# Fixed residues modulo 256 bytes for the large SBUF buffers of a one-core decoder step

## The chip, the cores and the metric

The kernel runs on one core of one Trainium2 chip. The metric is device time in microseconds (us) of one execution. TensorE (PE) does the matrix products; its weight loads are listed apart (PEld). VectorE (DVE), ScalarE (ACT) and GpSimd (POOL) do the element-wise work, and SyncE (SP) issues most of the DMAs.

## The reference

One layer of a hybrid decoder trunk on 256 prompt tokens and 64 sample tokens, 320 columns in all, in float32:

```python
h = rms_norm(x, attn_norm_g); z = h @ w_in       # [u | v | glu_a | glu_b | q | gates]
y_a = (gelu(u) * (tril(sgu_w) @ LN(gelu(v)) + sgu_b)) @ w_a_out
y_b = silu(LN(causal_dwconv(glu_a * sigmoid(glu_b)))) @ w_b_out
y_c = cross_attention(q, mem_k, mem_v) @ w_c_out
x = x + (g_A * y_a + g_B * y_b + g_C * y_c) @ w_o          # g = sigmoid(gates + b_gate)
x = x + square(relu(rms_norm(x, mlp_norm_g) @ w_up)) @ w_down
y = rms_norm(x, final_norm_g)
```

D_MODEL is 2048, the branches are 1024 wide and the MLP 8192. The keys and values of the prompt's memory come from `rms_norm(mem) @ w_mem_kv` (the "kv" stage); those of the samples are read from a cache. New keys and values, convolution states and the samples' normalised v rows are outputs too.

## The kernel before

Activations are held transposed, channels on the partitions and the 320 tokens along the row. Every large product takes float32 operands apart into a rounded part ("hi", type fp32r) and a remainder ("lo"), and adds three matmuls for each product of two 128-blocks: hi weights by hi activations, hi weights by lo activations, lo weights by hi activations. This document calls them a triple. They stand at L1307, L1308 and L1309 of the main loop, each with its own load of a 128x128 block of weights and 320 columns of activations as the moving operand:

```python
nc.tensor.matmul(a, hi[:, k, ms], xh, start=(kk == 0), stop=False)
nc.tensor.matmul(a, hi[:, k, ms], xl, start=False, stop=False)
nc.tensor.matmul(a, lo[:, k, ms], xh, start=False, stop=(last and k == 1))
```

The weights pass once, in 544 "halves" of 256 rows by 512 columns (512 KB). For each half, `load_to` (L199) has SP load a raw tile `wraw` (three buffers), ACT rounds it into `whi` (L222 where the norm's gain is multiplied in, L248 elsewhere) and DVE writes the remainder `wlo` (through the wrapper at L43); three buffers each. One half of a "T" product (512 of the 544) is four output blocks by two k-blocks, so eight triples, 24 matmuls. The other 32 halves are the kv stage (L1337 to L1339), where the weights are the moving operand, 512 columns, and the transposed memory `mh`/`ml` is loaded as the stationary one. The order of the stages is fixed by the list of groups: glu, q, kv, gate C, u, v, w_c_out, gate A with w_a_out, gate B with w_b_out, w_o, and then four times w_up and w_down. All other work (transposes, convolution taps on DVE, attention, norms) is put between the matmuls by hand, by half (`side`, `after`, `pace`), and the tile framework adds the semaphores.

Which buffers `operand` (L1021) gives as xh and xl depends on the stage: `hh`/`hl` for w_in and w_up, `ob` for w_c_out, `ya` for w_a_out, `yb` for w_b_out, `moh`/`mol` for w_o, `ah`/`al` for w_down. Under w_o, k-blocks 0 to 7 of `mol` lie in tag T5, and 8 to 15 in T7 (L1105).

Tiles come from one pool. A tag gets its place at its first use, one behind the other, each size rounded up to 32 bytes per partition, from byte 16,512 of the partition on. A row of 320 floats is 1280 bytes, five times 256, and blocks of weights start 512 bytes apart, so every operand of a matmul has the residue of its tile's start modulo 256. From the order and sizes in the program they are, before:

| buffers | tag | first byte | mod 256 |
|---|---|---|---|
| wraw | wraw | 61312 | 128 |
| hh, hl | HH, HL | 75232, 95712 | 224, 224 |
| whi, wlo | whi, wlo | 116192, 128480 | 224, 224 |
| ah, mh | T1 | 20352 | 128 |
| ya, ob (hi and lo), ml | T2 | 40832 | 128 |
| al, yb (hi, lo) | T4a, T4b | 177792, 188032 | 128, 128 |
| moh | T3a, T3b | 147072, 157312 | 128, 128 |
| mol, k-blocks 0 to 7 | T5 | 216096 | 32 |
| mol, k-blocks 8 to 15 | T7 | 205728 | 160 |

Of the kernel before, what the change touches and what calls it, by code (L numbers as in the profile page):

```python
# [10 lines left out]
F32R = mybir.dt.float32r  # L11
# [9 lines left out]
EPS = 1e-6  # L21
CONV_PACE = 0.75
WARM = 5
QUARTER = (0, 1)


# [22 lines left out]
def decoder_step_kernel(  # L49
# [26 lines left out]

    def tmp():
        return sb([128, NT], "tr", bufs=3)

    def f32(ap):  # L80
        return ap.bitcast(F32)
# [310 lines left out]
    def conv_setup():  # L392
        ident = S["ident"]
        cx = [sb([128, 4, 590], "T3a", name="cx0"), sb([128, 4, 590], "T3b", name="cx1")]
        S["cx"] = cx
        S["dc"] = sb([128, 8, NT], "T6", name="dc")
        hist = sb([120, 2, 1024], "T4a", name="hist")
        cwn = sb([31, 1024], "T4b", name="cwn")
        for g in range(2):
            nc.sync.dma_start(  # L400
                hist[:, g], state_conv[0, 4 * g:4 * g + 4].rearrange("b t c -> (b t) c")
            )
        nc.sync.dma_start(cwn, conv_w[0])
        nc.sync.dma_start(out_hist_s[0, :, 0:14, :], state_conv[0, :, 8:22, :])
        for t in cx:
            nc.gpsimd.memset(t[:, :, 0:30], 0.0)
        cw = sb([128, 8, 31], "cw")
        S["cw"] = cw
        steps = []

        def cw_step():
            p = ps_misc([128, 8, 64])
            for ct in range(8):
                nc.tensor.transpose(
                    p[:, ct, :31], cwn[:, 128 * ct:128 * (ct + 1)], ident[:31, :31]
                )
            nc.scalar.activation(cw, p[:, :, :31], AF.Copy)

        steps.append(cw_step)

        def hist_step(ct):
            p = ps_misc([128, 2, 256])
            for g in range(2):
                nc.tensor.transpose(
                    p[:, g, :120], hist[:, g, 128 * ct:128 * (ct + 1)], ident[:120, :120]
                )
            dst = cx[ct // 4][:, ct % 4, 286:590].rearrange("p (b w) -> p b w", w=38)
            for g in range(2):
                nc.scalar.activation(
                    dst[:, 4 * g:4 * g + 4, 0:30],  # L430
                    p[:, g, :120].rearrange("p (b t) -> p b t", t=30), AF.Copy,
                )

        for ct in range(8):
            steps.append(lambda ct=ct: hist_step(ct))
        return steps
# [113 lines left out]

    def yb_step(c):
        if c == 0:
            S["yb"] = [sb([128, 8, NT], t, F32R, name="yb") for t in ("T4a", "T4b")]
        split(S["yb"][0][:, c], S["yb"][1][:, c], S["dc"][:, c])


# [121 lines left out]
    def ya_step(g):  # L678
        if g == 0:
            flush()  # L680
            S["ya"] = sb([128, 2, 8, NT], "T2", F32R, name="ya")
        split(S["ya"][:, 0, g], S["ya"][:, 1, g], S["u"][:, g])


    def mem_load(i):
# [25 lines left out]

    def mem_tr_step(k):
        if k == 0:
            S["mh"] = sb([128, 16, 256], "T1", F32R, name="mh")
            S["ml"] = sb([128, 16, 256], "T2", F32R, name="ml")
        p = ps_misc([128, 2, 256])
        for t in range(2):
            nc.tensor.transpose(
                p[:, 0, 128 * t:128 * (t + 1)],
                S["mem"][k // 8][:, t, 128 * (k % 8):128 * (k % 8 + 1)], S["ident"],  # L720
            )
        split_scaled(S["mh"][:, k], S["ml"][:, k], p[:, 0], col("mem_g", k))
# [10 lines left out]
    def attn_prompt_steps(h):  # L733
        st = {}
        kt = (2 * h, 2 * h + 1)

        def scores():
            if h == 0:
                S["ob"] = sb([128, 2, 8, NT], "T2", F32R, name="ob")
            st["sc"] = ps_misc([128, 2, 256])  # L740
            for t in range(2):
                for j in range(2):
                    nc.tensor.matmul(  # L743
                        st["sc"][:, t], S["q"][:, kt[j], 128 * t:128 * (t + 1)],
                        S["kT"][:, kt[j]], start=(j == 0), stop=(j == 1),
                    )
            after(1, peak)
            after(2, soft)
            after(3, scale)

        def peak():
            mx = sb([128, 2], "mx", bufs=2)
            V.reduce_max(mx, st["sc"], axis=AX.X)
            st["nb"] = sb([128, 2], "nb", bufs=2)
            V.tensor_scalar(st["nb"], mx, -1.0 / 16, None, op0=ALU.mult)

        def soft():
            st["p"] = sb([128, 2, 256], "at", bufs=3)
            st["sm"] = sb([128, 2], "sm", bufs=2)
            for t in range(2):  # L760
                nc.scalar.activation(
                    st["p"][:, t], st["sc"][:, t], AF.Exp, bias=st["nb"][:, t:t + 1],
                    scale=1.0 / 16, accum_out=st["sm"][:, t:t + 1],
                )

        def scale():
            r = sb([128, 2], "rr", bufs=2)
            V.reciprocal(r, st["sm"])
            for t in range(2):
                V.tensor_scalar(st["p"][:, t], st["p"][:, t], r[:, t:t + 1], None, op0=ALU.mult)  # L770

        def tr():
            pp = ps_misc([128, 2, 256])
            for mt in range(2):
                for t in range(2):
                    nc.tensor.transpose(
                        pp[:, mt, 128 * t:128 * (t + 1)],
                        st["p"][:, t, 128 * mt:128 * (mt + 1)], S["ident"],
                    )
            st["pT"] = sb([128, 2, 256], "at", bufs=3)  # L780
            nc.scalar.activation(st["pT"], pp, AF.Copy)

        def pv():
            o = ps_misc([128, 2, 256])
            for j in range(2):
                for mt in range(2):
                    nc.tensor.matmul(  # L787
                        o[:, j], S["vn"][:, mt, 128 * kt[j]:128 * (kt[j] + 1)],
                        st["pT"][:, mt], start=(mt == 0), stop=(mt == 1),
                    )  # L790
            split(S["ob"][:, 0, 2 * h:2 * h + 2, 0:NP], S["ob"][:, 1, 2 * h:2 * h + 2, 0:NP], o)

        return [scores, tr, pv]

# [26 lines left out]
    def attn_sample_steps(g):  # L821
# [17 lines left out]
        def scores(b):  # L839
            sc = ps_misc([128, 512])  # L840
            for j in range(2):
                for h in range(4):
                    nc.tensor.matmul(  # L843
                        sc[32 * h:32 * h + 32, 0:256],
                        S["q"][:, 2 * h + j, NP + 32 * g:NP + 32 * g + 32],
                        st["kT"][:, 2 * h + j], start=(j == 0), stop=(j == 1),
                    )
            nb = sb([128, 2], "nb", bufs=2)
            sm = sb([128, 2], "sm", bufs=2)
            p = st["p"] = tmp()  # L850

            def peak():
                mx = sb([128, 2], "mx", bufs=2)
                V.reduce_max(mx[:, 0:1], sc[:, 0:256], axis=AX.X)
                V.tensor_scalar(nb[:, 0:1], mx[:, 0:1], -1.0 / 16, None, op0=ALU.mult)

            def soft():
                nc.scalar.activation(
                    p[:, 0:256], sc[:, 0:256], AF.Exp, bias=nb[:, 0:1], scale=1.0 / 16,
                    accum_out=sm[:, 0:1],  # L860
                )

            def scale():
                r = sb([128, 2], "rr", bufs=2)
                V.reciprocal(r[:, 0:1], sm[:, 0:1])
                V.tensor_scalar(
                    p[:, 0:256], p[:, 0:256], r[:, 0:1], S["mask"][:, b % 4:b % 4 + 1],
                    op0=ALU.mult, op1=ALU.mult,
                )

            after(1, peak)
            after(2, soft)
            after(3, scale)
# [31 lines left out]
        def fin():  # L905
# [5 lines left out]
            ob = S["ob"]  # L911
            for j in range(2):
                src = pp[:, j, 0:128].rearrange("p (h c) -> p h c", h=4)
                hi = ob[:, 0].rearrange("p (h j) t -> p h j t", j=2)[:, :, j, NP + 32 * g:NP + 32 * g + 32]
                lo = ob[:, 1].rearrange("p (h j) t -> p h j t", j=2)[:, :, j, NP + 32 * g:NP + 32 * g + 32]
                split(hi, lo, src)

        def T(b):
# [102 lines left out]
    def operand(key, kk):  # L1021
        kind = key[0]
        if kind in ("wA", "wC"):
            t = S[{"wA": "ya", "wC": "ob"}[kind]]
            return t[:, 0, kk], t[:, 1, kk]
        if kind == "wB":
            return S["yb"][0][:, kk], S["yb"][1][:, kk]
        if kind == "wo":
# [152 lines left out]


    with tc.manual_schedule():
        prologue()
        f = first

# [200 lines left out]
```

## Time and profile before

| what | value |
|---|---|
| median of 3 runs | 1999.29 us (1999.1 to 2005.92) |
| the profiled execution | 2000.53 us, of which its span is 1998.8 us |
| PE busy / PEld busy | 1976.0 us / 1933.9 us |
| DVE / ACT / POOL busy | 1194.4 / 821.0 / 32.7 us |
| HBM read | 311.48 MB, 159 GB/s over the span |

The page of the profile shows one profiled execution: busy time by engine, the span in 40 slices, the chain of work that ended last, and groups of instructions. The end of a matmul is modelled, so its duration (309 ns) says little; what a matmul costs in a dense stretch is the distance from its start to the next one's. That distance can be read in the list of instructions in order of time.

### The profile page before, as it was taken

Reading aid. Unit: us, or ns where it says so; the run is one execution under the profiler, and the core shown is the slowest. Engines: PE = TensorE matmul, PEld = TensorE weight load, DVE = VectorE, ACT = ScalarE, POOL = GpSimd, SP = SyncE. Lnnn points to the kernel's source line nnn. Section 1 sums busy time; section 2 is a strip of 40 time slices with the busy share of each in tenths; the row PEclk is TensorE's granted clock in tenths of the full one; section 3 lists DMA queues with packets and bytes.
Section 4 is the critical chain, followed back from the end, with each engine's and each line's share of the span. In section 5 each row is a group of like instructions: output and inputs, shape, how many; then the busy total and the mean of one; then the engine's idle time right before and its main releaser. Section 6 shows DMA issues by size and latency. Waiting matters only on the chain.

```text
span 1998.8 us, 32448 instructions
## 1 busy us (share of the span) xinstructions
PE 1976.0 (99%) x13316; PEld 1933.9 (97%) x13316; DVE 1194.4 (60%) x2079; ACT 821.0 (41%) x1185; POOL 32.7 (2%) x64
## 2 busy tenths in 40 slices
PE   9999999999999999999999999999999999999997
PEld 8999889889999999999999999999999999999997
DVE  5687787677788868655656554345434554445444
ACT  6454444445433445444444332233322333233332
POOL 0001000000200000000000000000000000000000
PEclk9999999999999999999999999999999999999998
DMA  6654665987644454544445544444444444444443
GB/s 212 192 148 141 208 200 121 208 225 205 217 150 136 148 150 146 152 156 151 139 162 168 152 144 149 158 149 147 149 157 148 149 142 153 158 148 147 145 152 106
DMA packets 189587, 319.25 MB, mean 160 GB/s; under 512 B 43377, under 2 KB 44105, under 8 KB 189302
## 3 DMA queue, kind: packets, MB, share of 16 engines
q1 hardware_dynamic: 184798, 302.56, 49.8%
q0 software_dynamic: 4640, 14.62, 2.1%
q8 instruction: 104, 1.70, 0.4%
q14 instruction: 45, 0.37, 0.1%
HBM read 311.48 MB, written 6.09 MB: 159 GB/s over the span
## 4 chain that ended last, share of the span: by engine, by line
PE 95%; DMA 2%; DVE 1%; ACT 0%; issue 0%; SPq 0%; DVEq 0%; ACTq 0%; POOLq 0%
PE acc L1307 29%; PE acc L1309 29%; PE acc L1308 29%; PE acc L1339 2%; PE acc L1338 1%; PE acc L1337 1%; DMA cache<-in_cache_mem_v_dram 1%; DMA wraw<-in_w_in_dram 1%; DVE wlo L43 0%; DMA cache<-in_cache_mem_k_dram 0%; PE misc L339 0%; PE misc L787 0%; PE misc L743 0%; PE misc L843 0%; PE acc L1285 0%; PE misc L893 0%
## 5 line engine op out<-in xcount | busy, mean ns | idle before, releaser
L1307 PE MATMUL acc<-hh,whi 128*128 128x320 f32 x2424 | 758.9, 313 | 0.0
L1309 PE MATMUL acc<-hh,wlo 128*128 128x320 f32 x2424 | 749.7, 309 | 0.0
L1308 PE MATMUL acc<-hl,whi 128*128 128x320 f32 x2424 | 749.6, 309 | 0.0
L43 DVE TENSOR_TENSOR wlo<-wraw,whi 128x1024 fp32r<-128x1024 f32 x368 | 448.7, 1222 | 427.4 <-ACT whi L248 427.3
L248 ACT ACTIVATE whi<-wraw 128x1024 fp32r<-128x1024 f32 x368 | 389.1, 1057 | 703.6 <-PE acc L1308 586.6
L1307 PEld LDWEIGHTS acc<-hh,whi 128*128 128x128 f32 x2424 | 455.8, 188 | 8.0 <-issue 6.6
L1308 PEld LDWEIGHTS acc<-hl,whi 128*128 128x128 f32 x2424 | 456.0, 188 | 0.4
L1309 PEld LDWEIGHTS acc<-hh,wlo 128*128 128x128 f32 x2424 | 455.6, 188 | 0.0
L222 ACT ACTIVATE whi<-wraw,vecs 128x512 fp32r<-128x512 f32 x352 | 236.5, 719 | 281.1 <-PE acc L1308 185.6
L1307 PE MATMUL acc<-ah,whi 128*128 128x320 f32 x1024 | 317.1, 310 | 0.0
L1308 PE MATMUL acc<-al,whi 128*128 128x320 f32 x1024 | 316.2, 309 | 0.0
L1309 PE MATMUL acc<-ah,wlo 128*128 128x320 f32 x1024 | 316.2, 309 | 0.0
L43 DVE SCALAR_TENSOR_TENSOR wlo<-wraw,vecs,whi 128x512 fp32r<-128x512 f32 x352 | 247.3, 745 | 71.2 <-ACT whi L222 70.4
L1308 PEld LDWEIGHTS acc<-al,whi 128*128 128x128 f32 x1024 | 192.5, 188 | 0.0
L1307 PEld LDWEIGHTS acc<-ah,whi 128*128 128x128 f32 x1024 | 192.5, 188 | 0.0
L1309 PEld LDWEIGHTS acc<-ah,wlo 128*128 128x128 f32 x1024 | 192.5, 188 | 0.0
L43 DVE SCALAR_TENSOR_TENSOR dc<-cx,cw,dc 128x256 f32<-128x256 f32 x480 | 153.0, 377 | 0.0
L43 DVE TENSOR_TENSOR res<-res,acc 128x320 f32<-128x320 f32 x80 | 39.0, 487 | 68.4 <-PE acc L1309 68.3
L1309 PE MATMUL acc<-moh,wlo 128*128 128x320 f32 x256 | 78.9, 308 | 0.0
L1307 PE MATMUL acc<-moh,whi 128*128 128x320 f32 x256 | 78.8, 308 | 0.0
L1308 PE MATMUL acc<-mol,whi 128*128 128x320 f32 x256 | 78.2, 306 | 0.0
L1039 ACT ACTIVATE ah<-tr 128x320 fp32r<-128x320 f32 x64 | 30.2, 472 | 67.3 <-DVE tr L43 67.3
(243 smaller groups left out, 1699.7 us busy)
## 6 DMA issues: line engine op xcount, KB each, us to landing
wraw<-in_w_in_dram SPq DMA_DIRECT2D x175, 512.0 KB, 4.0
wraw<-in_w_up_dram SPq DMA_DIRECT2D x128, 512.0 KB, 3.8
wraw<-in_w_down_dram SPq DMA_DIRECT2D x128, 512.0 KB, 3.6
wraw<-in_w_mem_kv_dram SPq DMA_DIRECT2D x32, 512.0 KB, 3.7
wraw<-in_w_o_dram SPq DMA_DIRECT2D x32, 512.0 KB, 3.7
cache<-in_cache_mem_k_dram SPq DMA_DIRECT2D x32, 256.0 KB, 6.4
cache<-in_cache_mem_v_dram POOLq DMA_DIRECT2D x8, 1024.0 KB, 7.3
wraw<-in_w_c_out_dram SPq DMA_DIRECT2D x16, 512.0 KB, 3.6
```

Source lines behind the costliest of these rows:

```text
L43: return fn(*args, **kw)
L222: nc.scalar.activation(hi, t, AF.Copy, scale=col("attn_g", 2 * h + k))
L248: nc.scalar.activation(parts[j][0], parts[j][1], AF.Copy)
L1039: nc.scalar.activation(out, in_, fn, **kw)
L1307: nc.tensor.matmul(a, hi[:, k, ms], xh, start=(kk == 0), stop=False)
L1308: nc.tensor.matmul(a, hi[:, k, ms], xl, start=False, stop=False)
L1309: nc.tensor.matmul(a, lo[:, k, ms], xh, start=False, stop=(last and k == 1))
L1337: nc.tensor.matmul(accs[t], mh, hi[:, k], start=(kk == 0), stop=False)
L1338: nc.tensor.matmul(accs[t], mh, lo[:, k], start=False, stop=False)
L1339: nc.tensor.matmul(accs[t], ml, hi[:, k], start=False, stop=(last and k == 1))
```

## The change

A new function `place` takes the large tags first, in a fixed order, right at the beginning, so that each keeps a chosen residue. Two helpers put a pad between the halves of a tile that holds hi and lo (40 floats, 160 bytes) or ahead of a hi part in a tag for lo ones (24 floats, 96 bytes). The small tiles of the softmax (`mx`, `nb`, `sm`, `rr`) become four parts of one tile `soft`, and the convolution's weights `cw` share the tag `rstd`. No instruction is added or removed by these edits.

```diff
+LO_HI, HI_LO, MEM_OFF = 40, 24, 0
...
+    def block(tag, name, off=0):
+        flat = sb([128, 8 * NT + off], tag, F32R, name=name)
+        return flat[:, off:].rearrange("p (k t) -> p k t", t=NT)
+    def both(tag, name):
+        flat = sb([128, 16 * NT + LO_HI], tag, F32R, name=name)
+        return [
+            flat[:, o:o + 8 * NT].rearrange("p (k t) -> p k t", t=NT)
+            for o in (0, 8 * NT + LO_HI)
+        ]
+    def mem_block(tag, name):
+        flat = sb([128, 16 * 256 + MEM_OFF], tag, F32R, name=name)
+        return flat[:, MEM_OFF:].rearrange("p (k t) -> p k t", t=256)
+    def place():
+        for tag, n, bufs in (
+            ("xss", 24, 1), ("whi", 1024, 3), ("wlo", 1024, 3), ("soft", 8, 2),
+            ("HL", 16 * NT, 1), ("T5", 8 * NT, 1), ("T7", 8 * NT, 1), ("T4b", 8 * NT, 1),
+            ("T4a", 8 * NT + HI_LO, 1), ("HH", 16 * NT, 1), ("T1", 16 * NT, 1),
+            ("T3a", 8 * NT, 1), ("T3b", 8 * NT, 1), ("T6", 8 * NT, 1),
+            ("T2", 16 * NT + LO_HI, 1),
+        ):
+            sb([128, n], tag, bufs=bufs, name="place")
...
-        cw = sb([128, 8, 31], "cw")
+        cw = sb([128, 8, 31], "rstd")
...
-            S["yb"] = [sb([128, 8, NT], t, F32R, name="yb") for t in ("T4a", "T4b")]
+            S["yb"] = [block("T4a", "yb", HI_LO), block("T4b", "yb")]
...
-            S["ya"] = sb([128, 2, 8, NT], "T2", F32R, name="ya")
-        split(S["ya"][:, 0, g], S["ya"][:, 1, g], S["u"][:, g])
+            S["ya"] = both("T2", "ya")
+        split(S["ya"][0][:, g], S["ya"][1][:, g], S["u"][:, g])
...
-            S["mh"] = sb([128, 16, 256], "T1", F32R, name="mh")
-            S["ml"] = sb([128, 16, 256], "T2", F32R, name="ml")
+            S["mh"] = mem_block("T1", "mh")
+            S["ml"] = mem_block("T2", "ml")
...
-                S["ob"] = sb([128, 2, 8, NT], "T2", F32R, name="ob")
+                S["ob"] = both("T2", "ob")
...
-            mx = sb([128, 2], "mx", bufs=2)
+            st["q"] = sb([128, 4, 2], "soft", bufs=2)
+            mx, st["nb"] = st["q"][:, 0], st["q"][:, 1]
...
     with tc.manual_schedule():
+        place()
         prologue()
```

Worked out from these sizes in the same way, the residues after are 224 for `whi` and `wlo` (bytes 16608 and 28896), 32 for `hl` (41248), T5, T7, T4b and T4a (61728, 71968, 82208, 92448; `yb`'s hi part begins 96 bytes into T4a, at 128), 128 for `hh` (102784), T1 (123264), T3a and T3b (143744, 153984) and T2 (174464), whose lo part begins at 184864, residue 32. `wraw` comes behind them and moves from residue 128 to 32.

More of the change, by code (lines that the diff above doesn't have):

```diff
@@ L751, in peak @@
         def peak():
-            mx = sb([128, 2], "mx", bufs=2)
+            st["q"] = sb([128, 4, 2], "soft", bufs=2)
+            mx, st["nb"] = st["q"][:, 0], st["q"][:, 1]
             V.reduce_max(mx, st["sc"], axis=AX.X)
-            st["nb"] = sb([128, 2], "nb", bufs=2)
             V.tensor_scalar(st["nb"], mx, -1.0 / 16, None, op0=ALU.mult)
@@ L758, in soft @@
             st["p"] = sb([128, 2, 256], "at", bufs=3)
-            st["sm"] = sb([128, 2], "sm", bufs=2)
+            st["sm"] = st["q"][:, 2]
             for t in range(2):
@@ L766, in scale @@
         def scale():
-            r = sb([128, 2], "rr", bufs=2)
+            r = st["q"][:, 3]
             V.reciprocal(r, st["sm"])
@@ L790, in pv @@
                     )
-            split(S["ob"][:, 0, 2 * h:2 * h + 2, 0:NP], S["ob"][:, 1, 2 * h:2 * h + 2, 0:NP], o)
+            split(S["ob"][0][:, 2 * h:2 * h + 2, 0:NP], S["ob"][1][:, 2 * h:2 * h + 2, 0:NP], o)
         return [scores, tr, pv]
@@ L847, in scores @@
                     )
-            nb = sb([128, 2], "nb", bufs=2)
-            sm = sb([128, 2], "sm", bufs=2)
+            q = sb([128, 4, 2], "soft", bufs=2)
+            mx, nb, sm, r = (q[:, i] for i in range(4))
             p = st["p"] = tmp()
             def peak():
-                mx = sb([128, 2], "mx", bufs=2)
                 V.reduce_max(mx[:, 0:1], sc[:, 0:256], axis=AX.X)
@@ L863, in scale @@
             def scale():
-                r = sb([128, 2], "rr", bufs=2)
                 V.reciprocal(r[:, 0:1], sm[:, 0:1])
@@ L913, in fin @@
                 src = pp[:, j, 0:128].rearrange("p (h c) -> p h c", h=4)
-                hi = ob[:, 0].rearrange("p (h j) t -> p h j t", j=2)[:, :, j, NP + 32 * g:NP + 32 * g + 32]
-                lo = ob[:, 1].rearrange("p (h j) t -> p h j t", j=2)[:, :, j, NP + 32 * g:NP + 32 * g + 32]
+                hi = ob[0].rearrange("p (h j) t -> p h j t", j=2)[:, :, j, NP + 32 * g:NP + 32 * g + 32]
+                lo = ob[1].rearrange("p (h j) t -> p h j t", j=2)[:, :, j, NP + 32 * g:NP + 32 * g + 32]
                 split(hi, lo, src)
@@ L1024, in operand @@
             t = S[{"wA": "ya", "wC": "ob"}[kind]]
-            return t[:, 0, kk], t[:, 1, kk]
+            return t[0][:, kk], t[1][:, kk]
         if kind == "wB":
```

## The prediction

> **What bounds the kernel now.** The page of the profile comes first: the span, the busy times, the clock slices and the chain that ended last.
>
> ```profile
> span 1998.8 us, 32448 instructions
> ...
> PE 1976.0 (99%) x13316; PEld 1933.9 (97%) x13316; DVE 1194.4 (60%) x2079; ACT 821.0 (41%) x1185; POOL 32.7 (2%) x64
> ...
> PEclk9999999999999999999999999999999999999998
> ...
> PE 95%; DMA 2%; DVE 1%; ACT 0%; issue 0%; SPq 0%; DVEq 0%; ACTq 0%; POOLq 0%
> PE acc L1307 29%; PE acc L1309 29%; PE acc L1308 29%; PE acc L1339 2%; PE acc L1338 1%; PE acc L1337 1%; DMA cache<-in_cache_mem_v_dram 1%; DMA wraw<-in_w_in_dram 1%; DVE wlo L43 0%; DMA cache<-in_cache_mem_k_dram 0%; PE misc L339 0%; PE misc L787 0%; PE misc L743 0%; PE misc L843 0%; PE acc L1285 0%; PE misc L893 0%
> ```
>
> The reader is to see that the chain runs on PE for 95% of the span, 87% of it in the three matmuls of the triple, at full granted clock. No other engine is near its limit over the span. So the time is the number of matmuls times the distance between their starts, and a change helps only if it shortens that distance. Busy time can't show this, since ends are modelled; the second view is the list of instructions in order of time, which has the starts. Here are the first matmuls of stretches in three stages: w_o (`moh`), w_up (`hh`) and w_down (`ah`).
>
> ```profile
> 966.05 0.31 PE L1307 MATMUL acc<-moh,whi 128*128 128x320 f32 x1
> 979.94 0.31 PE L1307 MATMUL acc<-moh,whi 128*128 128x320 f32 x1
> 993.92 0.31 PE L1307 MATMUL acc<-moh,whi 128*128 128x320 f32 x1
> 1007.78 0.31 PE L1307 MATMUL acc<-moh,whi 128*128 128x320 f32 x1
> 1021.76 0.31 PE L1307 MATMUL acc<-moh,whi 128*128 128x320 f32 x1
> 1035.62 0.31 PE L1307 MATMUL acc<-moh,whi 128*128 128x320 f32 x1
> 1049.60 0.31 PE L1307 MATMUL acc<-moh,whi 128*128 128x320 f32 x1
> 1063.46 0.31 PE L1307 MATMUL acc<-moh,whi 128*128 128x320 f32 x1
> 1092.06 0.31 PE L1307 MATMUL acc<-hh,whi 128*128 128x320 f32 x1
> 1176.54 0.31 PE L1307 MATMUL acc<-hh,whi 128*128 128x320 f32 x1
> 1204.70 0.31 PE L1307 MATMUL acc<-ah,whi 128*128 128x320 f32 x1
> 1289.18 0.31 PE L1307 MATMUL acc<-ah,whi 128*128 128x320 f32 x1
> ```
>
> By the loops of the code, four halves lie between neighbouring rows of w_o, that is 32 triples, and 24 halves between the two rows of w_up and of w_down, 192 triples. The w_up and w_down stretches last 84.48 us each: 84.48 / 192 = **440.0 ns per triple**. In w_o the stretches alternate: four of 13.89, 13.86, 13.86 and 13.86 us with three of 13.98 between them. That is 55.47 us for 4 x 32 triples, **433.4 ns** each, and 41.94 us for 3 x 32, 436.9 ns each. The shorter ones are k-blocks 0 to 7 and the longer ones 8 to 15, over and over. The form of the instruction is the same in all of these (128x320, same weights' buffers), and so is the work of the other engines within w_o. What differs between the two kinds of stretch is where `mol` lies: T5 at residue 32 against T7 at residue 160. What differs from w_up (hi and lo both at 224) and w_down (both at 128) is that there hi and lo have one and the same residue. So the start distance depends on the operands' residues: lo 96 bytes below hi gives 433.4, lo 32 above hi gives 436.9, equal residues give 440.0, with the weights at 224 each time.
>
> **The change part by part.** The first part is the residues. After it hi is at 128, lo at 32 and the weights at 224 in all T stages: the case of w_o's k-blocks 0 to 7. The bits above agree too, with one exception. Modulo 512, `hh` lies 160 above `whi` and `hl` 64 above it, as `moh` and `mol` do in the first half of w_o today, and the same holds for w_down, w_b_out and w_o; in `ya` and `ob` the lo part lies 256 bytes off that. How many triples there are is read from the groups of instructions by line and form, one row L1307 for each triple:
>
> ```profile
> L1307 PE MATMUL acc<-hh,whi 128*128 128x320 f32 x2424 | 758.9, 313 | 0.0
> L1307 PE MATMUL acc<-ah,whi 128*128 128x320 f32 x1024 | 317.1, 310 | 0.0
> L1307 PE MATMUL acc<-moh,whi 128*128 128x320 f32 x256 | 78.8, 308 | 0.0
> L1307 PE MATMUL acc<-ob,whi 128*128 128x320 f32 x128 | 40.2, 314 | 0.0
> L1307 PE MATMUL acc<-ya,whi 128*128 128x320 f32 x128 | 39.8, 311 | 0.0
> L1307 PE MATMUL acc<-yb,whi 128*128 128x320 f32 x128 | 39.5, 309 | 0.0
> ```
>
> Outside w_o that is 2424 + 1024 + 3 x 128 = 3832 triples. Each goes from 440.0 to 433.4, 6.6 ns less: 25.3 us. In w_o the 128 triples of k-blocks 8 to 15 go from 436.9 to 433.4: 0.4 us. The other 128 stay. Gross gain 25.7 us. For the 256 triples of `ya` and `ob`, with their lo part 256 bytes off, I take the full gain, since the alternation of even and odd k-blocks (1280 bytes apart, so 256 modulo 512) does not show in the stretches; the other end is no gain there, 1.7 us less.
>
> The kv stage keeps its residues (weights at 224, `mh` and `ml` at 128), so I cost it at nothing.
>
> What of the gain lands? Where PE waits for something else, a shorter triple only lengthens the wait. The chain in order of time names the places, and the busy time of L1307 in stretches says how many triples are there:
>
> ```profile
> 341.97 9.07 DMA wraw<-in_w_in_dram
> ...
> 352.20 8.17 DMA wraw<-in_w_in_dram
> ...
> 375.75 7.84 DMA cache<-in_cache_mem_k_dram
> ...
> 409.92 12.82 DMA cache<-in_cache_mem_v_dram x2
> ```
>
> ```profile
> 0.00:50.00 50.00, 20.12 (x62) 11.62 (x62) 1.00 0.69 212
> 350.00:400.00 50.00, 29.71 (x93) 17.85 (x92) 0.97 0.93 209
> 400.00:450.00 50.00, 29.71 (x95) 17.63 (x94) 1.00 0.84 226
> ```
>
> From about 342 to 423 us, in the attention on the samples' cache, the chain goes through transfers, with the DMA engines at 0.93 and 0.84 of their time. An estimate of the triples there is 93 + 95 x 23/50 = 137, so 0.9 us of gain that I take as lost; at the start of the kernel, where the inputs are loaded, 62 triples, 0.4 us. The upper end of the loss is all triples to 450 us, 188, and the start: 250 x 6.6 = 1.7 us. Net gain: 25.7 - 1.3 = **24.4 us**.
>
> Elsewhere a faster PE asks more of DVE, ACT and the loads. A row of the waits, two of the list by time and one of the DMA issues show the room:
>
> ```profile
> ACT whi L248 <- PE acc L1308: 586.6, 251, 3.5
> ```
>
> ```profile
> 1324.43 1.06 ACT L248 ACTIVATE whi<-wraw 128x1024 fp32r<-128x1024 f32 x1 [2.46 <-PE acc L1308]
> ```
>
> ```profile
> 1325.52 1.23 DVE L43 TENSOR_TENSOR wlo<-wraw,whi 128x1024 fp32r<-128x1024 f32 x1 [2.29 <-ACT whi L248]
> ```
>
> ```profile
> wraw<-in_w_up_dram SPq DMA_DIRECT2D x128, 512.0 KB, 3.8
> ```
>
> In a dense stretch ACT waits 2.46 us in each half of 3.52 us (8 x 440.0 ns) for PE to free a `whi` buffer, and DVE waits for ACT. A half gets 0.05 us shorter, far less than either wait, so neither becomes the bound. The raw buffers turn in three halves, 10.56 us. ACT begins at 1324.43, DVE ends at 1326.75, and a load that is issued then needs 3.8 us: 6.1 us of the 10.56 are used. This is also the cover for `wraw`'s own move to residue 32, which no row shows for these loads: from nothing up to the 4.4 us left, it costs nothing in the dense stretches; a gain there would be hidden as well. In the 81 us that transfers bound, a tenth longer on the 37.9 us of the four rows would be 3.8 us. I take nothing, since the bytes, the rows of 2048 bytes and their sources stay and only where a row begins moves, and keep 3.8 us for the range, on both sides of it.
>
> The other edits issue no instruction and no DMA. `soft` has two buffers, as `mx`, `nb`, `sm` and `rr` had; its third use writes first on DVE, behind the DVE operation that read the buffer last, so nothing new is waited for. `cw` in the tag of `rstd` is read by the convolution's taps on DVE, and the next writer of that tag is behind a DVE operation that follows all taps. Both I cost at nothing, with DVE's own order as the cover; if `soft` did hold something up, it would be at the start of a softmax in the attention, and a wait for one `wlo` operation (1.23 us, row above) at three of its 12 is 3.7 us, an estimate that I keep for the range.
>
> **Sum.** The profiled execution took 2000.5 us, 1.2 above the median of the runs shown, 1999.3. 2000.5 - 24.4 = 1976.1 for the former, and 1999.3 - 24.4 = **1974.9 us** for the median.
>
> **The rivals.**
> *No change.* The distance in w_o could come from something else than residues, such as where in SBUF T3 and T5 lie. For it: one stage only shows the short distance. Against it: `hh`, `ah`, `yb` lie far apart, and a triple in w_up and w_down is equal to 0.1 ns; within w_o the alternation follows `mol`'s place exactly. Time 1999.3. The Trainium skill, page "SBUF — State Buffer", section on the two separate sides, has a rule that comes to this: on the engines' side only the port pair that DVE and GpSimd share causes contention, and "PE, ACT, and DVE's dedicated pair never wait on anyone"; by that, where operands lie would be worth nothing and the sum would be 0. The trace disagrees: 433.4 and 440.0 ns for the same instruction.
>
> *Half of it.* The bits above 256 matter as well, and the new pairs fall into the case of w_o's k-blocks 8 to 15. Then a triple takes 436.9: 3832 x 3.1 = 11.9 us less, 1987.4. For it: two residues only are seen with hi and lo apart. Against it: modulo 512 most pairs repeat the better case.
>
> *Slower.* The distance is set by how the three reads (weights, lo, hi) fall against each other, and `hh`/`hl` or `ah`/`al` get a relation that no stage has today, worse than equal residues. The place is the 3832 triples. If it is as far above 440.0 as the best is below, 446.6, the price is +25.3 us, 2024.6. It decides from 440.0 + 10 000 ns / 3832 = 442.6 ns per triple on. Against it: no stage shows more than 440.0, whatever its residues.
>
> *A wait takes its place.* DVE, ACT or the loads become late: worked out above, within the range.
>
> **How the numbers follow.** The forecast has a chance of 0.80, half of it 0.07, no change 0.09, slower 0.04. The forecast's own range: the bounds of the unknown costs give a best case with all 25.7 us and up to 3.8 us from shorter transfers, 1999.3 - 29.5 = 1970; and a worst with 24.4 less 1.7 (`ya`, `ob`), 0.4 (more triples lost) and 3.8 (transfers or `soft`, not both), 18.5 net, 1981. That holds 0.80, so the range stays at 1970 to 1981. A measurement of this kernel tells about 0.5% (10 us) from no change; the forecast and half of it are beyond that: faster 0.87, same 0.09, slower 0.04.
>
> **What would show it.** Right: in the list by time, 24 halves of w_up and w_down without side work last 192 x 433.4 = 83.2 us in place of 84.48, and both kinds of stretch in w_o last 13.87; the stage of w_in too, and the counts of matmuls stay. The wait of ACT for PE drops by about 0.05 us in each half. If `ya` and `ob` stay at 440.0 while the rest shortens, bits above 256 count. If triples shorten and the time does not, the waits between 340 and 450 us have grown, and the transfers' landing times say whether `wraw`'s new residue is why. Triples at 440 or above would make the reason wrong, not only the size.

## The result and the profile after

| | before | after |
|---|---|---|
| median (lowest to highest), us | 2001.44 (1999.1 to 2005.92), 4 runs | 1984.26 (1981.1 to 1987.61), 4 runs |
| ratio to before, 95% interval | | 0.9904 [0.9883, 0.9925] |
| profiled execution, us | 2000.53, span 1998.8 | 1982.72, span 1981.0 |

The kernel became faster by 17.2 us by the medians and by 17.8 us by the spans. The forecast was 24.4 us and a time of 1974.9 us; the measured median lies 3.3 us above the range of 1970 to 1981. So the sign was right and the size was not. One later execution of the kernel after, the profiled one of the run after2 below, took 6173.71 us, three times any other, and is left out of everything that is worked out from that run.

The page of the kernel after, its first lines and the chain that ended last:

```profile
span 1981.0 us, 32448 instructions
...
PE 1955.5 (99%) x13316; PEld 1911.1 (96%) x13316; DVE 1194.1 (60%) x2079; ACT 821.2 (41%) x1185; POOL 32.8 (2%) x64
...
PEclk9999999999999999999999999999999999999999
...
PE 94%; DVE 3%; DMA 2%; ACT 0%; issue 0%; SPq 0%; DVEq 0%; ACTq 0%; POOLq 0%
```

The counts of instructions are those of before, and PE is still the bound. First the triples. The list of instructions by time, kernel after, with the first matmuls of stretches in w_c_out (ten triples), w_o (32 triples between rows) and w_down (192 triples):

```profile
575.06 0.31 PE L1336 MATMUL acc<-ob,whi 128*128 128x320 f32 x1
...
579.39 0.31 PE L1336 MATMUL acc<-ob,whi 128*128 128x320 f32 x1
...
962.16 0.31 PE L1336 MATMUL acc<-moh,whi 128*128 128x320 f32 x1
...
976.03 0.31 PE L1336 MATMUL acc<-moh,whi 128*128 128x320 f32 x1
...
989.90 0.31 PE L1336 MATMUL acc<-moh,whi 128*128 128x320 f32 x1
...
1198.45 0.31 PE L1336 MATMUL acc<-ah,whi 128*128 128x320 f32 x1
...
1281.65 0.31 PE L1336 MATMUL acc<-ah,whi 128*128 128x320 f32 x1
```

83.20 / 192 = 433.3 ns per triple in w_down, against 440.0 before. Both stretches in w_o last 13.87 us, so the alternation is gone, and `ob` takes 4.33 us for ten. The other engines have room as foreseen. In the waits of the kernel after (total in us, times, longest) ACT waits for PE 572.1 / 250 = 2.288 us a time, 0.05 us less than the 586.6 / 251 = 2.337 us of before:

```profile
ACT whi L278 <- PE acc L1337: 572.1, 250, 3.4
```

So every triple became as short as predicted. Where the rest of the gain went is seen from a place that cuts the kernel in two, the first matmul of w_c_out. Its row in the list by time, before and then after:

```profile
560.88 0.31 PE L1307 MATMUL acc<-ob,whi 128*128 128x320 f32 x1
```

```profile
562.29 0.31 PE L1336 MATMUL acc<-ob,whi 128*128 128x320 f32 x1
```

From there to the end of the span, before took 1998.8 - 560.88 = 1437.92 us and after takes 1981.0 - 562.29 = 1418.71 us. That is 19.2 us less. By the code 512 + 384 + 1024 + 1024 = 2944 of the 3832 triples (gates A and B, the three branch products, w_up, w_down) lie there, and 2944 x 6.6 + 0.4 = 19.8 us were due. **Ahead of it** 888 triples should have brought 5.9 us; with the 1.3 us of the prediction's losses 4.6 us were left. Instead after is 1.4 us late. So, in these two executions, 6.0 of the 6.6 us by which the spans fall short of the prediction are missing in the first 561 us.

The windows of 340 to 400 and 500 to 561 us (stretch, length, busy time of PE, PEld, DVE, ACT and POOL with counts, granted clock, DMA share, GB/s), before:

```profile
340.00:400.00 60.00, 56.95 (x399) 53.74 (x398) 44.96 (x94) 26.58 (x44) 0.74 (x1) 0.97 0.98 208
...
500.00:561.00 61.00, 60.01 (x456) 56.05 (x455) 43.38 (x105) 27.87 (x46) 10.80 (x17) 1.00 0.66 216
```

and after:

```profile
340.00:400.00 60.00, 56.91 (x402) 53.72 (x401) 45.74 (x94) 27.71 (x45) 0.74 (x1) 0.97 0.97 213
...
500.00:561.00 61.00, 58.14 (x438) 53.48 (x437) 41.41 (x102) 27.12 (x44) 10.81 (x17) 0.97 0.66 213
```

In the first stretch the faster PE gets nothing, as the prediction said: the DMA engines are busy for 0.97 of it. In the second one PE has 18 matmuls fewer on record than before in the same 61 us, and its clock is 0.97 in place of 1.00. The list by time shows the wait behind it: the attention's matmul waits for the samples' values from the cache, 0.99 us before (first fence) and 2.86 us after (second).

```profile
519.55 1.07 PE L893 MATMUL misc<-cache,at 128*32 128x256 f32 x16 [0.99 <-DMA cache<-in_cache_mem_v_dram]
```

```profile
511.25 1.94 PE L921 MATMUL misc<-cache,at 128*32 128x256 f32 x16 [2.86 <-DMA cache<-in_cache_mem_v_dram]
```

The 2.86 us are not all that this wait costs. The 16 matmuls behind it last 1.94 us, where those of before last 1.07, because the granted clock is at half. Three windows of the kernel after show it, with the columns as above:

```profile
508.00:511.00 3.00, 0.39 (x3) 0.12 (x1) 2.47 (x8) 0.00 (x0) 0.35 (x1) 1.00 0.69 203
511.00:514.40 3.40, 3.15 (x21) 1.88 (x22) 0.00 (x0) 0.00 (x0) 0.70 (x1) 0.50 0.78 304
514.40:517.40 3.00, 3.00 (x23) 3.00 (x22) 0.99 (x2) 1.60 (x3) 0.00 (x0) 1.00 0.73 257
```

The clock records of the trace have two such stretches of 3.4 us in the kernel after, at 384.7 and 511.0 us, and one in the kernel before, at 386.2 us, if the start and the end of the kernel are left out. At 0.50 a stretch of 3.4 us does the work of 1.7 us, so by this estimate the second one is up to 1.7 of the 6.0 us.

From 440 us on, the chain of the kernel before, by time, has one step on transfers (first fence), and that of the kernel after has two:

```profile
511.07 8.34 DMA cache<-in_cache_mem_v_dram
```

```profile
442.96 9.64 DMA wraw<-in_w_in_dram
...
501.67 9.53 DMA cache<-in_cache_mem_v_dram
```

So the question for the experiments is why transfers became later in the attention. The change also moved their destinations. `wraw` went from residue 128 to 32, and, since `cache_load` and `mem_load` put their tiles into the tags T7 and T4a, those tiles went from 160 and 128 to 32 as well. Two smaller loads into these tags, `hist` and `fg`, moved with them; the runs on landing places leave them where the change puts them.

### The profile page after: what moved, and what is told of

The parts are those of the page before. It is cut to its first block, busy times and chain, and to the rows that moved or that the text cites. A ratio compares the mean times of both kernels' runs of the same rounds, so it can differ in the third digit from the quotient of the medians.

```text
span 1981.0 us, 32448 instructions
## 1 busy us (share of the span) xinstructions
PE 1955.5 (99%) x13316; PEld 1911.1 (96%) x13316; DVE 1194.1 (60%) x2079; ACT 821.2 (41%) x1185; POOL 32.8 (2%) x64
## 4 chain that ended last, share of the span: by engine, by line
PE 94%; DVE 3%; DMA 2%; ACT 0%; issue 0%; SPq 0%; DVEq 0%; ACTq 0%; POOLq 0%
PE acc L1336 29%; PE acc L1338 29%; PE acc L1337 28%; PE acc L1368 2%; PE acc L1367 2%; PE acc L1366 1%; DMA wraw<-in_w_in_dram 1%; DVE wlo L44 1%; DMA cache<-in_cache_mem_v_dram 1%; DVE dc L44 1%; DMA cache<-in_cache_mem_k_dram 0%; DVE kTb L44 0%; PE misc L369 0%; PE misc L921 0%; PE misc L817 0%; PE misc L773 0%
## 5 line engine op out<-in xcount | busy, mean ns | idle before, releaser
L1337 PE MATMUL acc<-hl,whi 128*128 128x320 f32 x2424 | 739.5, 305 | 0.0
L278 ACT ACTIVATE whi<-wraw 128x1024 fp32r<-128x1024 f32 x368 | 389.6, 1059 | 688.2 <-PE acc L1337 572.1
L1337 PE MATMUL acc<-al,whi 128*128 128x320 f32 x1024 | 311.6, 304 | 0.0
L44 DVE SCALAR_TENSOR_TENSOR wlo<-wraw,vecs,whi 128x512 fp32r<-128x512 f32 x352 | 247.1, 743 | 72.4 <-ACT whi L252 71.9
L44 DVE SCALAR_TENSOR_TENSOR dc<-cx,rstd,dc 128x256 f32<-128x256 f32 x480 | 152.9, 377 | 0.0
```

The source lines that it names most:

```text
L44: return fn(*args, **kw)
L278: nc.scalar.activation(parts[j][0], parts[j][1], AF.Copy)
```

## The experiments

Each ratio below is to runs of the kernel before on the same chip, whose medians lay between 2000.88 and 2002.04 us.

**Three explanations for the missing 6 us** are told apart first: the loads land worse where they now land; the shared `soft` tile holds up the softmax; or a faster PE alone meets the same transfers earlier, whatever lies where.

*all32.* Both pads go, so hi and lo lie at 32 in all T stages, with the weights at 224 and all loads' tiles at 32. What is left of the change is the order of the buffers, without the shorter triple.

```diff
-LO_HI, HI_LO, MEM_OFF = 40, 24, 0
+LO_HI, HI_LO, MEM_OFF = 0, 0, 0
```

> The changed kernel with the pads set to 0, so that hi and lo both lie at residue 32 in every stage, weights at 224, and all loads land where they do in the changed kernel (wraw, cache and mem at 32). It has the new placement without the difference between hi and lo. Theory W (the loss is waits: PE arrives earlier at transfers whose time is fixed): equal residues give 440.0 ns per triple and the kernel takes the time of before, ratio 1.000, within 0.003. Theory P (the new destinations make transfers land later): 440.0 ns per triple and the stalls of the changed kernel, so about 8 us above before, ratio 1.004. If residue 32 itself, not the difference, is what helps: 433 ns and ratio 0.991.

Measured: 2005.42 us, ratio 1.0019 [1.0009, 1.0028]. Two rows of w_down in the list by time of this kernel, 192 triples apart:

```profile
1213.46 0.31 PE L1336 MATMUL acc<-ah,whi 128*128 128x320 f32 x1
...
1297.94 0.31 PE L1336 MATMUL acc<-ah,whi 128*128 128x320 f32 x1
```

84.48 / 192 = 440.0 ns: equal residues of hi and lo give the triple of before, at 32 as at 128 and 224. And with the triple of before the kernel is slower than before by 0.19%, 3.7 us by the medians. The interval lies above 1, so something in the new places costs time without a faster PE. It is half of the 8 us that the expectation gave to worse landing places alone, and it lies inside the 0.003 that it left to a faster PE that meets the same transfers earlier, so this run does not rule the latter out for the rest. In this kernel the tiles of the inputs (T1 and T2) also land at 32 in place of 128, which they do not in the change. In the traces that is little: the kv stage begins at 196.8 us against 196.2 before, and w_c_out at 568.4 against 560.9.

*dest128.* The change, with the three kinds of landing tiles put back: `wraw` at 128 by a pad, the `mem` and `cache` tiles at 160 in T7 and 128 in T4a.

```diff
+    def landing(i, name):
+        off = (32, 24)[i]
+        flat = sb([128, 2048 + off], ("T7", "T4a")[i], name=name)
+        return flat[:, off:].rearrange("p (t c) -> p t c", t=2)
...
+        sb([128, 24], "pad", name="place")
...
-        t = sb([128, 2, 1024], ("T7", "T4a")[i], name="mem")
+        t = landing(i, "mem")
...
-        t = sb([128, 2, 1024], ("T7", "T4a")[j % 2], name="cache")
+        t = landing(j % 2, "cache")
```

> The changed kernel with the loads' destinations as before: wraw and the tiles of T4a that receive mem and the cache at residue 128, those of T7 at 160; operands as in the changed kernel (hi 128, lo 32, weights 224). Theory P: the 8 us that are missing come back, ratio to before 0.988 (about 1976 us). Theory W: as the changed kernel, ratio 0.990 to 0.992, stalls between 360 and 530 us as long as there.

Measured: 1979.0 us, ratio 0.9884 [0.9870, 0.9897]. The span of the profiled execution is 1973.8 us, 25.0 below that of before. The group of `ob` at the start of w_c_out (count, minimum, median and longest duration in ns, first and last start in the stretch up to 575 us):

```profile
L1342 PE MATMUL acc<-ob,whi x43: 307/308/393, 555.2 to 574.8; 128*128 128x320 f32 x43
```

w_c_out begins at 555.2 us, 5.7 us ahead of before. That is nearly the whole gain that the 888 triples ahead of it can bring.

*soft4.* The softmax's four small tiles apart again, as before the change.

```diff
-            st["q"] = sb([128, 4, 2], "soft", bufs=2)
-            mx, st["nb"] = st["q"][:, 0], st["q"][:, 1]
+            mx = sb([128, 2], "mx", bufs=2)
...
+            st["nb"] = sb([128, 2], "nb", bufs=2)
...
```

> The changed kernel with the softmax's four small tiles apart again (mx, nb, sm, rr, two buffers each) in place of soft. Theory S (the shared tile holds up a step of the attention): up to 4 us faster than the changed kernel, ratio to before 0.988 to 0.989. Theories W and P: as the changed kernel, 0.990 to 0.992.

Measured: 1982.21 us, ratio 0.9906 [0.9892, 0.9921]; w_c_out begins at 564.0 us, no earlier than in the kernel after (562.3). The 0.988 to 0.989 that a wait at the shared tile would have given lie outside the interval, so the shared tile is not the cause.

*after2.* The kernel of the change once more, on the chip of these three.

> The changed kernel once more, as the partner of the three others on the same chip and for a second trace of its stalls. Theory V (chance: landing times vary from run to run, and the first profile drew long ones): its stalls at the sample attention differ from those of the first profile by microseconds, and the ratio comes out nearer 0.988. Theories W and P: stalls of the same size at the same places, ratio 0.990 to 0.991.

Measured: a median of 1981.5 us over four executions, ratio 0.9896 [0.9880, 0.9911]. It gives no second trace of the stalls, so it does not say whether chance drew long ones in the first profile; soft4, with the same landing places, begins w_c_out as late. The interval of dest128 overlaps this one. But after2 and soft4 together have nine executions with the change's landing places on this chip, which average 1982.4 us, and dest128's four average 1978.6. If the thirteen times are dealt at random into groups of nine and four, a gap of 3.9 us comes up in 0.6% of the deals. That counts the soft tiles as worth nothing. The next runs look for firmer evidence.

**Which load, and which residue?** *wraw128* puts only `wraw` back to 128 (the pad of dest128 alone), *cache128* only the `mem` and `cache` tiles (the rest of dest128's edit), and *dest0* puts all of them at residue 0, with `off = (56, 56)[i]` and `sb([128, 56], "pad", name="place")`.

> The changed kernel with only wraw moved back to residue 128 (one pad of 96 bytes ahead of it); the tiles that receive mem and the cache stay at 32. dest128, with both moved back, measured a ratio to before of 0.9884. If it is wraw's 2048-byte rows whose landing got longer: 0.9885 and short stalls at the sample attention. If it is the cache's rows: as the changed kernel, 0.990 to 0.9905.

> The changed kernel with only the tiles that receive mem and the cache moved back (T4a 128, T7 160); wraw stays at 32. If it is the cache's rows of 256 and 4096 bytes: 0.9885, and the mean of the 256-byte packets in the sample attention falls from 27.9 to about 26.5 ns. If it is wraw: as the changed kernel, 0.990 to 0.9905, packets of 256 bytes unchanged.

> The changed kernel with wraw and all tiles that receive mem and the cache at residue 0. If a load is the faster the rounder its destination (32 worse than 128, 0 at least as good as 128, and T7 at 160 half of the remaining loss): stalls at the sample attention below those of dest128, ratio to before 0.986 to 0.988. If only residue 32 is bad: as dest128, 0.9884. Triples 433.3 ns in both.

Measured: wraw128 1979.31 us, 0.9898 [0.9882, 0.9915]; cache128 1981.32 us, 0.9896 [0.9881, 0.9910]; dest0 1976.08 us, 0.9875 [0.9861, 0.9890]. The first two can't be told from each other or from the kernel after, and w_c_out begins at 558.2 us in wraw128, at 561.1 in cache128 and at 554.8 in dest0. So which of the moved tiles carries the loss from 128 and 160 to 32 is not shown: only both moved back together, dest128, brought most of it back, by its trace. Residue 0 for all has the lowest ratio. What differs most is seen in the trace's records of DMA packets. The keys of the samples' cache come in rows of 256 bytes, some 31 thousand packets between 340 and 530 us. The mean time of one, worked out from those records (in ns, not a view of the page):

```
destination of the cache tiles        kernels and mean ns of one 256-byte packet
128 and 160                           before 27.2, dest128 26.2, cache128 27.2
32                                    after 27.9, all32 28.9, soft4 28.8, wraw128 28.7, wraw0 28.0
0                                     dest0 20.3, cache0 20.4, all32dest0 20.5, best 20.0
```

31,000 packets on 16 engines make 1,940 for each, so 28 against 20.4 ns is 14.7 us of each engine's time in a stretch of 190 us. At 32 the packets are dearer than at 128 and 160 by 0.7 to 2.7 ns, that is 1.4 to 5 us of each engine. How much of that reaches the kernel's time is not shown by it: cache128 has the 27.2 ns of before and the ratio of the kernel after. The Trainium skill, page "DMA: Bandwidth & Descriptors", section "How a descriptor splits into AXI transactions", says for reads that a descriptor is cut at 256-byte boundaries into transactions and that one which starts off a boundary pays for the unused bytes ahead of it. Worked out by that page for 256 bytes, an estimate, it is 8 beats at residue 0, 9 at 32, 12 at 128 and 13 at 160. The trace agrees that 0 is the cheapest; it does not agree on the order of the others, 28 to 29 ns at 32 against 26 to 27 ns at 128 and 160, and here the measurement decides. The page speaks of reads, and these rows are written into SBUF at the residue in question.

*all32dest0.* all32 with dest0's landing tiles: triples of 440.0 ns as before, only the destinations differ from all32.

> all32 (hi and lo both at 32, weights at 224, triples 440 ns) with wraw and the tiles that receive mem and the cache at residue 0. It changes the destinations of the loads alone, against all32 (ratio to before 1.0019) and, with 128 and 160 there, before. If destinations act by themselves: 256-byte packets near 20 ns, ratio about 0.998 to 0.999, 3 us under before and 6 to 7 under all32. If they only count together with the faster triples: 1.000 to 1.002.

Measured: 1999.81 us, ratio 0.9991 [0.9979, 1.0002], against all32's 1.0019 [1.0009, 1.0028]. The intervals are apart by themselves. The groups of `ob` at the start of w_c_out, all32 and then all32dest0:

```profile
L1336 PE MATMUL acc<-ob,whi x13: 307/308/393, 568.4 to 574.6; 128*128 128x320 f32 x13
```

```profile
L1342 PE MATMUL acc<-ob,whi x40: 307/308/394, 556.4 to 575.0; 128*128 128x320 f32 x40
```

The same triples, the same order of work, and w_c_out begins 12.0 us earlier in these two executions (0.28%, 5.6 us, by the ratios, from 10 and 12 executions; the all32 that was profiled is the slowest of its ten). Its trace has two stretches of 3.4 us at half the clock, that of all32dest0 none. That the landing places move the time is thereby shown, and shown without any change in the triples.

*cache0 and wraw0.* The change, with only the `mem` and `cache` tiles at residue 0 (`off = (56, 56)[i]`, `wraw` stays at 32), and with only `wraw` at 0 (the pad of dest0 alone).

> The changed kernel with the tiles that receive mem and the cache at residue 0, wraw left at 32. dest0, with both at 0, measured 0.9875 against 0.990 of the changed kernel. If the cache's 256-byte rows carry the loss: ratio 0.987 to 0.988, packets of 256 bytes near 20 ns in the sample attention. If wraw carries it: 0.990.

> The changed kernel with wraw at residue 0, the tiles that receive mem and the cache left at 32. If wraw carries the loss: ratio 0.987 to 0.988 with 256-byte packets still at 28 ns. If the cache's rows carry it: 0.990. If each carries a part: both kernels between 0.988 and 0.9895.

Measured: cache0 **1973.72 us**, ratio 0.9862 [0.9847, 0.9876]; wraw0 1979.9 us, ratio 0.9895 [0.9880, 0.9910]. So residue 0 pays for the `mem` and `cache` tiles and not for `wraw`: moving `wraw` gives what the kernel after gives, moving those tiles alone gives 0.33% more than that. The `mem` tiles, which are read before the kv stage, can have little part in it: kv begins at 194.5 us in cache0 and at 195.4 in the kernel after. The DMA view of 340 to 530 us shows the same from the other side, first the kernel after, then cache0 (queue: packets, MB, share of the 16 engines' time; issues: count, KB each, median us from issue to landing):

```profile
q1 hardware_dynamic: 43711, 31.53, 71.9%
...
wraw<-in_w_in_dram SPq DMA_DIRECT2D x45, 512.0 KB, 5.9
...
cache<-in_cache_mem_k_dram SPq DMA_DIRECT2D x29, 256.0 KB, 6.7
```

```profile
q1 hardware_dynamic: 43881, 32.30, 63.4%
...
wraw<-in_w_in_dram SPq DMA_DIRECT2D x47, 512.0 KB, 5.1
...
cache<-in_cache_mem_k_dram SPq DMA_DIRECT2D x28, 256.0 KB, 5.9
```

As many packets take 63.4% in place of 71.9%. The weights land in 5.1 us in place of 5.9, although `wraw` is at 32 in both. In the same stretch they took 6.0 us in wraw0 and 5.8 in wraw128, so `wraw`'s own residue is not what delayed them. The cache at 32 is not proven to be it either: before had 5.2, but so had maphi (below), with the cache at 32. The windows of cache0 and its first matmul of w_c_out:

```profile
340.00:400.00 60.00, 59.83 (x435) 56.71 (x434) 49.55 (x103) 31.20 (x52) 0.74 (x1) 1.00 0.83 216
```

```profile
553.68 0.31 PE L1341 MATMUL acc<-ob,whi 128*128 128x320 f32 x1
```

Between 340 and 400 us PE does 435 matmuls, 33 more than in the kernel after, at a clock of 1.00 in place of 0.97 and with the DMA engines at 0.83 in place of 0.97. w_c_out begins 8.6 us earlier than after and 7.2 us earlier than before, more than the 5.9 us of the triples; before landed its cache off residue 0 as well. The chain of cache0 by time, 340 to 530 us, has no step on `wraw` or on the keys any more:

```profile
402.80 13.06 DMA cache<-in_cache_mem_v_dram x2
...
495.05 7.07 DMA cache<-in_cache_mem_v_dram
...
503.57 9.08 DMA cache<-in_cache_mem_v_dram
```

**Which residues make the short triple?** Three kernels, with one timed execution each, give every stage its own pair, by a list of `take(tag, size, buffers, residue)` calls in `place` that pad up to the residue asked for. *map224* keeps the weights at 224 and hi at 128 and varies lo; *maphi* keeps lo at 32 and varies hi; *mapw* moves the weights to 96. A piece of mapw's list:

```diff
+        take("HL", 16 * NT, 1, 160)
...
+        take("T5", 8 * NT, 1, 192)
+        take("HH", 16 * NT, 1, 0)
...
+        take("T3a", 8 * NT, 1, 32)
...
+        take("whi", 1024, 3, 96)
+        take("wlo", 1024, 3, 96)
```

> A map: hi at 128 and the weights at 224 in all stages, lo at a residue of its own in each: hl 0, al 64 (k-blocks 0 to 7) and 96 (8 to 15), mol 160 and 192, the lo part of ya and ob 224, yb's 96. Theory D (only lo minus hi counts, modulo 64 bytes): differences of a multiple of 64 (0, 64, 192) give 440 ns per triple, odd multiples of 32 (96, 160, 224) give 433 to 437. Theory L (the value of the residue counts, lo ahead of hi by less than 128 bytes is good): a graded list, 0, 64 and 96 below 440, 160 to 224 between 436 and 440.

> A map of hi: lo at 32 and weights at 224 everywhere, hi at a residue of its own in each stage: hh 0, ah 64, moh 96 (k-blocks 0 to 7) and 160 (8 to 15), the hi part of ya and ob 192, yb's 224. If lo's place against the weights alone counts: 433.3 ns per triple everywhere. If hi has to lie 96 above lo as well: 440 everywhere, since 128 does not occur here.

> The weights at 96 instead of 224, 128 bytes lower. hh 0 with hl 160: the changed kernel's residues all moved by 128. ah 128 with al 32 (k-blocks 0 to 7): its activations as they are, the weights moved. al 160 (8 to 15): as w_o's second half before, weights moved. moh 32 with mol 192, and 96 with 0: lo minus hi as in the changed kernel, at other places against the weights. ya and ob 64 with 224, yb 192 with 160. If only differences count and the period is 256: hh/hl 433.3. If the period is 128: hh/hl 433.3 and also ah with 32. If the residues count for themselves and not against the weights: ah with 32 433.3, hh/hl not.

Measured: map224 2003.55, maphi 1995.96, mapw 1983.3 us. What counts are the triples, by the starts in the list by time as above. With hi and lo given as their distance above the weights' residue, modulo 256:

| hi - w | lo - w | ns per triple | where |
|---|---|---|---|
| 160 | 64 | 433.3 | after, all stages; mapw w_in and w_up, with all three moved by 128 |
| 0 | 64 | 433.3 | maphi, `yb` |
| 32 | 64 | 436.7; 436.6 | maphi, `hh`; mapw, `ah` with `al` in T4b |
| 192 | 64 | 436.8 | maphi, `moh` in T3b |
| 64, 96, 128, 224 | 64 | 440.0 to 440.1 | all32; maphi `ah`, `moh` in T3a, `ya` and `ob`; mapw `yb` (96) |
| 160 | 192 | 436.9 | before, w_o k-blocks 8 to 15; map224 the same |
| 160 | 0, 32, 96, 128, 160, 224 | 440.0 to 440.2 | map224; before, w_down (160) |
| 0 | 0 | 440.0 | before, w_up |
| 32; 0; 224 | 192; 160; 128 | 440.2; 439.8; 439.9 to 440.0 | mapw, w_down with `al` in T4a; w_o k-blocks 8 to 15; `ya` and `ob` |
| 192 | 96 | 442.1 | mapw, w_o k-blocks 0 to 7 |

The last is the worst pair met, in the list by time of mapw, 32 triples apart:

```profile
955.82 0.30 PE L1352 MATMUL acc<-moh,whi 128*128 128x320 f32 x1
...
969.96 0.31 PE L1352 MATMUL acc<-moh,whi 128*128 128x320 f32 x1
```

14.14 us / 32 = 442 ns. In map224 the only triple below 440.0 was at lo 160, and hi follows a pattern of its own in maphi, so neither of the two simple rules that map224 tried, nor either of maphi's, holds for all rows. Of mapw's three, the first agrees: the distances to the weights count, with a period of 256. What does hold: a stage is fastest where lo lies 64 above the weights and hi 160 (or 0) above them; moved as a whole by 128 the three keep their time; hi and lo being unequal is not enough. The reason for these particular distances was not found.

*best.* Weights at 96, hi at 0, lo at 160, all loads' tiles at 0, and the kv stage's `mh` at 128 and `ml` at 64, where mapw's kv triples had taken 692 to 695 ns in place of 700.

> All residues of the operands as far from the weights as in the changed kernel, the whole moved by 128 (weights 96, hi 0, lo 160), so that the inputs' tiles in T1 and T2 begin at 0 as well; wraw, mem and cache at 0; in the kv stage mh at 128 and ml at 64, as far from the weights as in the map with the weights at 96 (692 to 695 ns per triple in place of 700). Triples 433.3 ns. If all parts add up: about 1 us under dest0, ratio 0.9865 to 0.9875. If not: as dest0, 0.9875.

Measured: 1973.68 us, ratio 0.9857 [0.9841, 0.9874]. Triples of 433.3 ns and kv triples of 691 to 695 ns are there (128 x 5 to 8 ns would be 0.6 to 1 us), yet it can't be told from cache0. cache0 and best both beat the two kernels of this study; cache0 is the smaller edit.

## Why the prediction was right and where it failed

- **Bound and lever: right.** PE's starts set the time, and the residues of the operands set their distance. The other engines kept their room: ACT's wait for PE shrank by the 0.05 us foreseen.
- **The size per triple: right in every stage.** It was 433.3 ns against the 433.4 taken over from w_o's better half. `ya` and `ob`, for which the other end was no gain, got the whole of it. w_o's k-blocks 8 to 15 did too, and kv stayed at 700 ns.
- **Gain behind 561 us: right.** 19.2 us of the 19.8 due.
- **What failed: "This is also the cover for `wraw`'s own move to residue 32 [...] I take nothing, since the bytes, the rows of 2048 bytes and their sources stay and only where a row begins moves".** The step looked at one load and asked only about rows of 2048 bytes. The `mem` and `cache` tiles, which move to residue 32 with T7 and T4a, stand in no sentence of it, and they carry rows of 256 bytes into the one stretch that transfers bound. all32 measured what the new places cost with the triple unchanged, 1.0019 [1.0009, 1.0028], some 3.7 us, and all32dest0 that the landing places alone move the time, 0.9991 [0.9979, 1.0002]. The prediction's bound of 3.8 us "from shorter transfers" or longer ones had the right size; the forecast put zero in its place. For `wraw` itself no cost is seen: at 0 and at 128 (wraw0, 0.9895; wraw128, 0.9898) the ratio can't be told from the change's. But cache128 (0.9896) can't either, so which tile carries the loss from 128 and 160 to 32 stays open; what is shown for the `mem` and `cache` tiles is the gain at residue 0.
- **The loss in waits was mis-sized.** A loss of 1.3 us was taken for both the start and the attention; by the profiled execution the 5.9 us due ahead of w_c_out did not come and 1.4 us more went, 7.3 us in all. The place of the waits was off too: the attention's waits past 450 us (501 to 511 us) grew, not only those from 342 to 423. The chain of before has a transfer there too, 8.34 us from 511.07 on (shown above), and the prediction's list of the chain stops short of it. No term of the sum is for the granted clock, which stood at half once more than before for 3.4 us behind such a wait, by the estimate above up to 1.7 us. With the old destinations (dest128) the span falls by 25.0 us and the ratio is 0.9884 [0.9870, 0.9897], which holds the predicted 24.4 us (0.9878). That all the rest of the gap is the destinations is argued from this, and from the stretch in which it lies; the intervals of dest128 and after2 overlap. The gap itself is not known well: by after2's ratio the change gained 20.8 us (17.8 to 24.0), 3.6 short of the forecast, by the first comparison 17.2.
- **The base was low.** The time was counted from the median of three runs, 1999.3; four later medians lie between 2000.9 and 2002.0. That is some 2 of the 9.4 us between 1974.9 and 1984.26.
- **`soft` and `cw` at nothing: right for `soft`**, by soft4; `cw` was not tried alone.
- **The rivals.** No change and half of it fell with 433.3 ns. With it falls what the prediction drew from the Trainium skill, page "SBUF — State Buffer", section on the two separate sides, that where operands lie would be worth nothing. The page's own sentence is on one engine waiting for another, which these distances do not test. The slower case did not come about, but it is no invention: mapw's 442.1 ns is a relation worse than equal residues. The wait that takes the place was the one that came, with a cause which the prediction named for `wraw` only.

Open are why these residues matter to the matmuls, which of the tiles moved to 32 costs the time there, and whether best is any better than cache0.

## What to carry to other kernels

When buffers are moved to suit one engine, list every tile in the moved tags with all who write it, the transfers above all, and give each a line of the sum. Try tiles that receive short rows on multiples of 256 bytes first, above all where the DMA engines are the bound: here, with rows of 256 bytes, that was worth 0.33%. For a stream of matmuls, compare start distances of the same form between stages before any model of them: here the stage that was 1.5% faster told where its operands should lie.

## What the runs showed of the hardware that was not expected

- A 256-byte packet into SBUF took 20.0 to 20.5 ns on average at residue 0 and 26.2 to 28.9 ns at 32, 128 or 160, in the same stretch.
- The time of a triple depends on hi and lo separately, each against the weights, with levels near 433.3, 436.7, 440.0 and 442.1 ns.
- The kv stage, with 512 columns, reacts as well: 700 ns per triple with weights at 224 and `mh`, `ml` at 128; 691 to 695 ns with 96, 128 and 64.
- The granted clock falls to 0.50 for 3.4 us behind a long wait of PE. Between 20 and 1960 us, the traces of the fifteen kernels have 15 such stretches. Each begins between 0.5 us before and 1.5 us after the end of a PE wait of 1.7 to 3.1 us (386.2 us before; 384.7 and 511.0 us in the kernel after), so the wait comes first. All waits above 2.43 us between 40 and 1960 us had one; of the shorter ones some had none (2.43 us in map224, 2.16 in dest0). The traces of dest128, dest0, cache0 and all32dest0 have none of these stretches; after, all32, soft4, cache128 and best have two each.
